# Split-heads rotary embedding: the cos table loaded from SyncE's queue, and TensorE's wait for sin moved behind the spreading of cos

## The chip, the cores and the metric

The kernel runs on one core of a Trainium2 chip. The metric is the device time of one execution in microseconds (us). The engines are TensorE (PE), VectorE (DVE), ScalarE (ACT), GpSimd (POOL) and SyncE (SP); ScalarE and SyncE each have a DMA queue here, which the profile calls q10 and q1, and both are served by the same 16 DMA engines.

## What is computed

```python
def reference(x, cos, sin, num_heads):          # x: 16 x 512 x 1024, cos and sin: 512 x 32, 16 heads
    x = x.reshape(batch, seq, num_heads, head_dim)             # head_dim 64
    x1, x2 = x[..., :half_dim], x[..., half_dim:]              # half_dim 32
    cos, sin = cos[None, :, None, :], sin[None, :, None, :]
    return np.concatenate([x1 * cos - x2 * sin, x1 * sin + x2 * cos], axis=-1)
```

All is float32. 33.55 MB of x are read and as much is written; each of the two tables has 64 KB.

## The kernel before

The 8192 rows of x (batch times sequence) are cut into eight tiles of 1024 rows. A tile has 128 partitions with eight consecutive rows each, 4 MB in all. A step u of the kernel treats one row of each partition, 128 x 1024 numbers, so there are 64 steps. The tiles live in a ring of 40 such rows in SBUF (x_sb, 160 KB of a partition); tiles 5 to 7 reuse the places of tiles 0 to 2, and the results overwrite x in place before they are stored.

For a step, VectorE multiplies x by cos into PSUM (t1_ps, line 347). GpSimd, for most steps, multiplies x with its halves swapped by the sines, the first half with its sign changed, into SBUF (t2_sb, lines 303 and 305); for some steps VectorE does this too (line 340). The sum of the two is made in one of two ways, set by the list PE2: VectorE adds them (line 356), or TensorE adds t2 to t1 in PSUM by a matmul with the identity (line 265) and ScalarE copies the result back (line 227).

Each engine has its own program, and semaphores join them. **ScalarE** (lines 205 to 232) issues the DMA of the first half tile of x (2 MB), then those of cos and sin, then five more x loads: the second half of tile 0 and tiles 1 to 4. It then forms the selection matrix (line 215) from an identity that GpSimd makes, and later the sine tables (lines 222, 223). The loads of tiles 5 to 7 (`late`) are issued by ScalarE behind fixed steps (BEHIND) and wait until the stores of the rows that they overwrite have landed. **SyncE** (lines 195 to 203) issues nothing but the ten stores: each waits for the sums of its rows. **TensorE** (lines 234 to 273) first writes zeros to its banks, then waits for the selection, for cos and for sin, and spreads the two tables with the selection, so that each of the 128 partitions has the table rows of its eight rows: the cos group goes to tab_ps, the sin group to a bank of t1_ps (line 248). One increment of sem_t follows both groups. VectorE's first product, ScalarE's sine copies and through them GpSimd's first product wait for it. There is one tile size, so SIZES has a single entry.

The spreading loop, which fixes the order of the two groups:

```python
for n in SIZES:
    for c, to in enumerate((c_ps[n], raw_sin[n])):
        for k in range(n // R1):
            ins = pe.matmul(...)
    ins.then_inc(sem_t, 1)
```

Of the kernel before, what the change touches and what calls it, by code (L numbers as in the profile page):

```python
# [6 lines left out]
def bass_split_heads_rope_kernel(  # L7
# [14 lines left out]
    R1 = seq // P  # L22
# [27 lines left out]
    SIZES = sorted({t[0] for t in TILES})  # L50
# [40 lines left out]
    with ExitStack() as stack:  # L91
        x_sb = stack.enter_context(nc.sbuf_tensor([P, RING, H, 2, HALF], fp32))
        t2_sb = stack.enter_context(nc.sbuf_tensor([P, NT2, H, 2, HALF], fp32))
        stage = stack.enter_context(nc.sbuf_tensor([P, 2, R1 * HALF], fp32))
# [13 lines left out]
        sem_cos = stack.enter_context(nc.semaphore("cos"))  # L108
        sem_sin = stack.enter_context(nc.semaphore("sin"))
# [37 lines left out]
        def in_dram(flat, t, o, m):  # L147
            n = TILES[t][0]
            run = flat[first_row[t] * P:(first_row[t] + n) * P, :].rearrange("(p r) d -> p (r d)", r=n)
            return run[:, o * dim:(o + m) * dim]  # L150

        def place_of(u):
            t, r = rows[u]
            return TILES[t][1] + r

        def in_sbuf(t, o, m):
            k = TILES[t][1] + o
            return x_sb[:, k:k + m].rearrange("p n h t d -> p (n h t d)")
# [14 lines left out]
        def wait_added(eng, u):  # L173
            if n_pe[u]:
                eng.wait_ge(sem_a, n_pe[u])
            if n_comb[u]:
                eng.wait_ge(sem_v, n_comb[u])  # L177
# [9 lines left out]
        def load(eng, i):  # L187
            t, o, m = loads[i]
            eng.dma_start(in_sbuf(t, o, m), in_dram(xf, t, o, m)).then_inc(sem_in[i], 16)  # L189

        def wait_landed(eng, t, r):
            if (t, r) in load_at:
                eng.wait_ge(sem_in[load_at[t, r]], 16)

        def on_sync(sp):
            for u in range(NU):
                if u not in store_after:
                    continue
                k = store_after[u]
                t, o, m = stores[k]  # L200
                wait_added(sp, u)
                sp.dma_start(in_dram(of, t, o, m), in_sbuf(t, o, m)).then_inc(sem_out.get(k, sem_rest), 16)
            sp.wait_ge(sem_rest, 16 * (len(stores) - len(awaited)))

        def on_scalar(ae):
            early = [i for i in range(len(loads)) if i not in late]
            for i in early:
                load(ae, i)
                if i == 0:
                    for c, (table, sem) in enumerate(((cos, sem_cos), (sin, sem_sin))):  # L210
                        ae.dma_start(stage[:, c, :], table.rearrange("(s r) d -> s (r d)", r=R1)).then_inc(sem, 16)  # L211
            ae.wait_ge(sem_i, 2)
            for n in SIZES:
                m = n // R1
                ae.activation(  # L215
                    pick[n][:],
                    ident[:].rearrange("q (s k) -> q k s", k=m)[:, :, None, :].broadcast_to([P, m, m, P // m]),
                    COPY,
                ).then_inc(sem_g, 1)
            for i, n in enumerate(SIZES):  # L220
                ae.wait_ge(sem_t, i + 1)
                ae.activation(s_sb[n][:, :, 0, :], raw_sin[n], COPY, scale=-1.0)  # L222
                ae.activation(s_sb[n][:, :, 1, :], raw_sin[n], COPY).then_inc(sem_s, 1)  # L223
            for u in range(NU):
                if PE2[u]:
                    ae.wait_ge(sem_e, n_pe[u])
                    ae.activation(xs[:, place_of(u), :], t1_ps[:, u % NT1, :], COPY).then_inc(sem_a, 1)  # L227
                for i in late:
                    if BEHIND[i] == u:
                        for j in TILES[loads[i][0]][4]:  # L230
                            ae.wait_ge(sem_out[j], 16)
                        load(ae, i)

        def on_tensor(pe):
            pe.wait_ge(sem_z, 1)
            for k in range(NT1):
                for b in range(EH):
                    pe.matmul(  # L238
                        t1_ps[:, k, b * BANK:(b + 1) * BANK], zero[:, 0:P], zero[:], start=True, stop=True
                    ).then_inc(sem_w, 1)  # L240
            pe.wait_ge(sem_g, len(SIZES))
            pe.wait_ge(sem_cos, 16)
            pe.wait_ge(sem_sin, 16)
            pe.wait_ge(sem_w, NT1 * EH)
            for n in SIZES:
                for c, to in enumerate((c_ps[n], raw_sin[n])):
                    for k in range(n // R1):
                        ins = pe.matmul(  # L248
                            to[:, k * R1:(k + 1) * R1, :].rearrange("p r d -> p (r d)"),
                            pick[n][:, k].rearrange("q b s -> q (b s)"),  # L250
                            stage[:, c, :],
                            start=c == 0,
                            stop=True,
                            skip_group_check=c == 1,
                        )
                ins.then_inc(sem_t, 1)
            for u in range(NU):
                if not PE2[u]:
                    continue
                if TWO[u - 1]:  # L260
                    pe.wait_ge(sem_q[(u - 1) % NT2], made[u - 1])
                pe.wait_ge(sem_q[u % NT2], made[u])
                t2 = t2_sb[:, u % NT2, :, :, :].rearrange("p h t d -> p (h t d)")
                for b in range(EH):
                    ins = pe.matmul(  # L265
                        t1_ps[:, u % NT1, b * BANK:(b + 1) * BANK],
                        ident[:],
                        t2[:, b * BANK:(b + 1) * BANK],
                        start=False,
                        stop=True,  # L270
                        skip_group_check=True,
                    )
                ins.then_inc(sem_e, 1)
# [40 lines left out]
        def on_vector(ve):  # L314
# [48 lines left out]
            for u in range(NU + LEAD):  # L363
# [6 lines left out]
                if u >= LEAD and not ahead and not PE2[u - LEAD]:  # L370
                    comb(u - LEAD)

        on_sync(nc.sync)
        on_scalar(nc.scalar)
        on_gpsimd(nc.gpsimd)
        on_tensor(nc.tensor)
        on_vector(nc.vector)

# [32 lines left out]
```

## Time and profile before

| what | value |
|---|---|
| time, median of 3 runs | 160.91 us (160.89 to 161.15) |
| the profiled execution: time | 161.04 us |
| its span, first to last instruction | 159.8 us |
| DVE busy | 134.1 us (84%) |
| POOL busy | 126.5 us (79%) |
| PE busy | 56.3 us (35%) |
| ACT busy | 21.8 us (14%) |
| moved by DMA | 67.25 MB, mean 421 GB/s |

A profile comes from one execution, so its durations belong to 161.04 us. Busy time counts instructions of an engine; issuing a DMA and waiting for a semaphore are not counted. The row of 40 digits for an engine shows the busy tenths of 40 equal slices of the span, some 4 us each; the DMA row shows the mean of the 16 DMA engines in the same way. In lines of the timeline the columns are start, duration, engine, line, operation, output and inputs, number of instructions, and in brackets the idle time of the engine before them with what ended it. An "ACTq" or "SPq" line is the issue of a DMA on that engine's queue, not the transfer. The time from issue to landing holds the wait behind other transfers. The trace also records each DMA packet with its start and duration, and when each transfer's semaphore was raised.

### The profile page before, as it was taken

How to read it: one execution, taken by the hardware profiler on the slowest of the kernel's cores; microseconds unless marked ns; L12 is line 12 of the kernel's file. 1: busy time of each engine (PE TensorE's matmuls, PEld its weight loads, DVE VectorE, ACT ScalarE, POOL GpSimd, SP SyncE). 2: the span in 40 equal slices, each digit the busy share in tenths (PEclk: the TensorE clock that was granted, in tenths of full speed). 3: DMA queues.
4: the chain of work that ended last, by engine and by line, in shares of the span. 5: the costliest groups of instructions: out<-in, count | busy, mean ns of one | idle time of the engine just before them, and what ended most of it. 6: DMA issues, size and time to landing. Idle time of an engine off the chain costs nothing.

```text
span 159.8 us, 449 instructions
## 1 busy us (share of the span) xinstructions
PE 56.3 (35%) x90; PEld 19.6 (12%) x90; DVE 134.1 (84%) x121; ACT 21.8 (14%) x23; POOL 126.5 (79%) x40
## 2 busy tenths in 40 slices
PE   6050007744407740788066407740575000000000
PEld 1040002111102110222021102110220000000000
DVE  0028997999999999998999999999799987999500
ACT  0410000331300330022203300330022000000000
POOL 1009999999999999999999999956999289990000
PEclk9999999999985899557659985899557655555555
DMA  5999998999999999999999999999999999999996
GB/s 172 418 426 459 435 476 336 422 414 418 500 406 455 435 427 394 420 492 402 394 500 410 402 484 427 402 427 484 402 394 509 402 402 476 435 402 443 406 439 287
DMA packets 3025, 67.25 MB, mean 421 GB/s; under 512 B 336, under 2 KB 592, under 8 KB 592
## 3 DMA queue, kind: packets, MB, share of 16 engines
q10 hardware_dynamic: 1584, 33.69, 49.8%
q1 hardware_dynamic: 1440, 33.56, 48.8%
q14 instruction: 1, 0.01, 0.0%
HBM read 33.69 MB, written 33.55 MB: 421 GB/s over the span
## 4 chain that ended last, share of the span: by engine, by line
DMA 45%; DVE 34%; POOL 11%; PE 1%; issue 1%; ACTq 1%; ACT 0%; SPq 0%; POOLq 0%
DMA x_sb<-in_x_dram 21%; DMA out_dram<-x_sb 20%; DVE t_ps L347 18%; DVE x_sb L356 14%; POOL t_sb L305 6%; POOL t_sb L166 5%; DMA stage<-in_sin_dram 4%; DVE t_sb L166 3%; PE tab_ps L248 1%; PE t_ps L248 1%; ACTq L211 0%; ACT sine L222 0%; ACTq L189 0%; ACT sine L223 0%; SPq L177 0%
## 5 line engine op out<-in xcount | busy, mean ns | idle before, releaser
L305 POOL TENSOR_TENSOR t_sb<-x_sb,sine 128x2048 f32<-128x2048 f32 x22 | 99.0, 4524 | 6.6 <-DMA x_sb<-in_x_dram 6.6
L347 DVE TENSOR_TENSOR t_ps<-x_sb,tab_ps 128x1024 f32<-128x1024 f32 x64 | 76.8, 1221 | 11.3 <-PE t_ps L248 9.9
L265 PE MATMUL t_ps<-t_sb,ident 128*128 128x512 f32 x76 | 51.5, 818 | 59.4 <-DVE t_ps L347 38.6
L356 DVE TENSOR_TENSOR x_sb<-t_ps,t_sb 128x1024 f32<-128x1024 f32 x45 | 54.7, 1219 | 3.7 <-POOL t_sb L305 3.0
L166 POOL TENSOR_TENSOR t_sb<-x_sb,sine 128x1024 f32<-128x1024 f32 (+1 forms) x12 | 27.6, 2307 | 10.4 <-ACT sine L223 10.4
L227 ACT ACTIVATE x_sb<-t_ps 128x1024 f32<-128x1024 f32 x19 | 19.4, 1023 | 91.9 <-PE t_ps L265 89.9
L265 PEld LDWEIGHTS t_ps<-t_sb,ident 128*128 128x128 f32 x76 | 17.1, 250 | 92.7 <-issue 53.6
L166 DVE TENSOR_TENSOR t_sb<-x_sb,tab_ps 128x1024 f32<-128x1024 f32 (+1 forms) x9 | 10.1, 1124 | 0.0
L238 PE MATMUL t_ps<-zero 128*128 128x512 bf16 x6 | 2.7, 630 | 1.3 <-DVE zero L315 1.3
L248 PE MATMUL tab_ps<-stage,chosen 128*128 128x128 f32 x4 | 1.2, 454 | 4.9 <-DMA stage<-in_sin_dram 4.9
L215 ACT ACT_TABLE_LOAD x1 | 1.3, 1283 | 4.8 <-issue 4.8
L248 PEld LDWEIGHTS tab_ps<-stage,chosen 128*128 128x128 f32 x4 | 0.9, 322 | 5.8 <-issue 5.8
L248 PE MATMUL t_ps<-stage,chosen 128*128 128x128 f32 x4 | 1.1, 421 | 0.0
L315 DVE MEMSET zero<- 128x256 uint32 x1 | 0.3, 272 | 0.9 <-PEq L393 0.9
L238 PEld LDWEIGHTS t_ps<-zero 128*128 128x128 bf16 x6 | 0.7, 137 | 2.4 <-DVE zero L315 1.2
L222 ACT ACTIVATE sine<-t_ps 128x256 f32<-128x256 f32 x1 | 0.4, 383 | 4.4 <-PE t_ps L248 4.4
L248 PEld LDWEIGHTS t_ps<-stage,chosen 128*128 128x128 f32 x4 | 1.0, 333 | 0.0
L276 POOL MEMSET ident<- 128x128 f32 x1 | 0.2, 204 | 0.3 <-POOLq L393 0.3
L215 ACT ACTIVATE chosen<-ident 128x256 f32<-128x256 f32 x1 | 0.4, 429 | 0.0
L223 ACT ACTIVATE sine<-t_ps 128x256 f32<-128x256 f32 x1 | 0.4, 378 | 0.0
L278 POOL TENSOR_SCALAR_AFFINE_SELECT ident<-ident 128x128 f32<-128x128 f32 x1 | 0.3, 292 | 0.1
L393 POOL MEMSET const-float32-0.0<- 128x1 f32 x1 | 0.1, 98 | 0.3 <-issue 0.3
(5 smaller groups left out, 0.7 us busy)
## 6 DMA issues: line engine op xcount, KB each, us to landing
x_sb<-in_x_dram ACTq DMA_DIRECT2D x7, 4096.0 KB, 33.2
out_dram<-x_sb SPq DMA_DIRECT2D x6, 4096.0 KB, 30.2
out_dram<-x_sb SPq DMA_DIRECT2D x4, 2048.0 KB, 16.4
x_sb<-in_x_dram ACTq DMA_DIRECT2D x2, 2048.0 KB, 9.4
stage<-in_cos_dram ACTq DMA_DIRECT2D x1, 64.0 KB, 7.2
stage<-in_sin_dram ACTq DMA_DIRECT2D x1, 64.0 KB, 7.0
```

Source lines behind the costliest of these rows:

```text
L166: return eng.tensor_tensor(t2_sb[:, u % NT2, a:b, :, :], swapped(place_of(u))[:, a:b], table[:, None, :, :].broadcast_to([P, b - a, 2, HALF]),
L215: ae.activation(pick[n][:], ident[:].rearrange("q (s k) -> q k s", k=m)[:, :, None, :].broadcast_to([P, m, m, P // m]), COPY,).then_inc(se ...
L222: ae.activation(s_sb[n][:, :, 0, :], raw_sin[n], COPY, scale=-1.0)
L223: ae.activation(s_sb[n][:, :, 1, :], raw_sin[n], COPY).then_inc(sem_s, 1)
L227: ae.activation(xs[:, place_of(u), :], t1_ps[:, u % NT1, :], COPY).then_inc(sem_a, 1)
L238: pe.matmul(t1_ps[:, k, b * BANK:(b + 1) * BANK], zero[:, 0:P], zero[:], start=True, stop=True).then_inc(sem_w, 1)
L248: ins = pe.matmul(to[:, k * R1:(k + 1) * R1, :].rearrange("p r d -> p (r d)"), pick[n][:, k].rearrange("q b s -> q (b s)"), stage[:, c, :] ...
L265: ins = pe.matmul(t1_ps[:, u % NT1, b * BANK:(b + 1) * BANK], ident[:], t2[:, b * BANK:(b + 1) * BANK], start=False, stop=True, skip_group ...
L278: pl.affine_select(out=ident[:], in_=ident[:], compare_op=mybir.AluOpType.is_equal, fill=0.0, base=0, pattern=[[-1, P]], channel_multiplier=1,
L305: pl.tensor_tensor(t2_sb[:, u % NT2:u % NT2 + 2].rearrange("p n h t d -> p (n h) t d"), x_sb[:, k:k + 2, :, ::-1, :].rearrange("p n h t d ...
L347: ve.tensor_tensor(t1_ps[:, u % NT1, :].rearrange("p (h d) -> p h d", d=HALF), x_sb[:, k, :, :, :].rearrange("p h t d -> p (h t) d"), c_ps ...
L356: ve.tensor_tensor(xs[:, place_of(u), :], t1_ps[:, u % NT1, :], t2_sb[:, u % NT2, :, :, :].rearrange("p h t d -> p (h t d)"), add,).then_i ...
```

## The change

The helper load_table issues the DMA of one table. SyncE calls it for cos before its loop of stores. ScalarE issues only sin behind the first half tile of x. TensorE still waits for the selection, for cos and for its zeros before the first group, but for sin only ahead of the second group. Semaphores, sizes, the order of x loads and of stores, and all arithmetic stay.

```diff
+        def load_table(eng, c):
+            table, sem = ((cos, sem_cos), (sin, sem_sin))[c]
+            eng.dma_start(stage[:, c, :], table.rearrange("(s r) d -> s (r d)", r=R1)).then_inc(sem, 16)
+
         def on_sync(sp):
+            load_table(sp, 0)
             for u in range(NU):
                 if u not in store_after:
                     continue
@@ on_scalar
             for i in early:
                 load(ae, i)
                 if i == 0:
-                    for c, (table, sem) in enumerate(((cos, sem_cos), (sin, sem_sin))):
-                        ae.dma_start(stage[:, c, :], table.rearrange("(s r) d -> s (r d)", r=R1)).then_inc(sem, 16)
+                    load_table(ae, 1)
@@ on_tensor
             pe.wait_ge(sem_g, len(SIZES))
             pe.wait_ge(sem_cos, 16)
-            pe.wait_ge(sem_sin, 16)
             pe.wait_ge(sem_w, NT1 * EH)
             for n in SIZES:
                 for c, to in enumerate((c_ps[n], raw_sin[n])):
+                    if c == 1 and n == SIZES[0]:
+                        pe.wait_ge(sem_sin, 16)
                     for k in range(n // R1):
```

## Prediction

> **What bounds the kernel now.** I read the page's slices and queue table first, then busy time in short windows, then the timeline of the first 12 us, then the waits for x late in the run. The page says that the DMA engines are full nearly from end to end.
>
> ```profile
> span 159.8 us, 449 instructions
> ...
> DVE  0028997999999999998999999999799987999500
> ACT  0410000331300330022203300330022000000000
> POOL 1009999999999999999999999956999289990000
> ...
> DMA  5999998999999999999999999999999999999996
> ...
> q10 hardware_dynamic: 1584, 33.69, 49.8%
> q1 hardware_dynamic: 1440, 33.56, 48.8%
> ```
>
> Queue q10 is ScalarE's (loads), q1 SyncE's (stores). Together they fill 98.6% of 159.8 us on 16 engines: 157.6 us, so an engine is idle for 2.2 us on the mean. VectorE, busy 134.1 us, does nothing in the last 9. Where the 2.2 us lie is shown by the windows (columns: stretch, its length, busy of PE, PEld, DVE, ACT, POOL, granted clock, DMA share, GB/s).
>
> ```profile
> 0.00:2.00 2.00, 0.75 (x2) 0.28 (x3) 0.27 (x1) 0.00 (x0) 0.70 (x6) 1.00 0.45 90
> 2.00:4.00 2.00, 1.99 (x5) 0.45 (x3) 0.00 (x0) 0.00 (x0) 0.00 (x0) 1.00 0.68 254
> 4.00:6.00 2.00, 0.00 (x0) 0.00 (x0) 0.00 (x0) 1.18 (x1) 0.00 (x0) 1.00 1.04 442
> ...
> 150.00:154.00 4.00, 0.00 (x0) 0.00 (x0) 0.02 (x1) 0.00 (x0) 0.00 (x0) 0.50 1.02 438
> 154.00:158.00 4.00, 0.00 (x0) 0.00 (x0) 0.00 (x0) 0.00 (x0) 0.00 (x0) 0.50 0.97 414
> 158.00:160.00 2.00, 0.00 (x0) 0.00 (x0) 0.00 (x0) 0.00 (x0) 0.00 (x0) 0.50 0.33 139
> ```
>
> Nothing moves before 1.82 us, when the first packet of the first x load starts (packet records of the trace); by 4 us the engines run at 430 GB/s, and they do so until 158. After the last arithmetic at 150.0 us DMA is still full: the last store, issued at 150.10, stands behind the one before, which lands at 154.93, and itself lands at 159.76, a time of 4.83 us for 2 MB. So the end is set by when the DMA engines start, by 67.25 MB, and by what they lose on the way. The page's chain of waits runs through VectorE for a third of the span, but it names what came last, and the windows show that an earlier store would find the engines occupied.
>
> **The change, part by part.** Durations are of the profiled execution: span 159.8, time 161.04, so 1.25 us lie outside the span. Its time is 0.13 above the median 160.91.
>
> The start today, from the timeline:
>
> ```profile
> 0.80 0.38 ACTq L189 DMA_DIRECT2D x_sb<-in_x_dram  x1
> 1.21 0.46 ACTq L211 DMA_DIRECT2D stage<-in_cos_dram  x1
> 1.69 0.45 ACTq L211 DMA_DIRECT2D stage<-in_sin_dram  x1
> 2.17 2.62 ACTq L189 DMA_DIRECT2D x_sb<-in_x_dram  x5
> 4.82 1.28 ACT L215 ACT_TABLE_LOAD   x1 [4.82 <-issue]
> 6.12 0.43 ACT L215 ACTIVATE chosen<-ident 128x256 f32<-128x256 f32 x1
> 8.90 1.19 PE L248 MATMUL tab_ps<-stage,chosen 128*128 128x128 f32 x4 [4.91 <-DMA stage<-in_sin_dram]
> 9.89 1.06 PE L248 MATMUL t_ps<-stage,chosen 128*128 128x128 f32 x4
> 10.98 0.38 ACT L222 ACTIVATE sine<-t_ps 128x256 f32<-128x256 f32 x1 [4.44 <-PE t_ps L248]
> 11.79 8.72 POOL L166 TENSOR_TENSOR t_sb<-x_sb,sine 128x1024 f32<-128x1024 f32 x4 [10.43 <-ACT sine L223]
> ```
>
> (a) **ScalarE issues one DMA less**: 0.48 us (1.21 to 1.69). Sin, five x loads, the table load and the spread of the selection move up by it: the selection is ready at 6.55 - 0.48 = 6.07. The x loads behind the first only queue earlier behind full engines: 0.
>
> (b) **SyncE issues cos first.** SyncE is released with the others (0.72 us) and has nothing to do until its first store at 21.81, so its 0.46 us cost no work. The first x packet started 1.02 us after its issue began; cos, issued at 0.80, should start at 1.82 to 1.90, beside x. Its cost to DMA: the 256 packets of 512 B of both tables took 27 ns each, so cos takes 128 x 27 / 16 = 0.22 us of each engine, wherever it stands. Taken before or between x packets instead of behind them: 0.
>
> What the trace of before does not show is two queues that open at the same moment. Best case: cos fills time that the engines lose at the start anyway. The 16 first packets start between 1.82 and 2.87 (mean 2.05) and the packets before 4 us take 0.65 us per engine above the steady 0.611 us for 16 KB; all of this saved would be -0.65. Worst case: the first x load waits for the whole cos issue, +0.46. A second row bounds a queue that opens: around the first store, in 24 to 26 us, load packets took 0.31 us per engine longer than the steady 1.213 us; the two together would be +0.77. I take 0, because the nearest row, the tables' own 0.22 us, only changes place, and the costs of opening exist once already.
>
> (c) **TensorE's wait for sin moves behind the cos matmuls.** The cos group (1.19 us) can run from 6.1, or from when cos lands, at latest some 7 us (eight packets on each engine, alternating with x packets of 0.61 us, from 1.9), and ends by 8.2. Sin still stands behind 2 MB of x in q10, so it lands at 8.65, as today, or up to 0.22 earlier. Behind the new wait are queued the four sin matmuls and then all adds of TensorE; VectorE's first product waits for them too. From 8.65: 0.25 to the matmul, 1.06 for the group, 0.02, two copies to 0.66 later, 0.14 to GpSimd: its first product starts at 10.8, not 11.79. VectorE moves from 11.09 to 10.1. **The front of the arithmetic gains 1.0 us**, the cos group that no longer stands behind sin; the first store is issued at 20.8, not 21.81.
>
> (d) **Where that 1.0 us goes.** Loads and stores share full engines, so a store that starts earlier takes time from the loads. Stores in q1 wait for one another: the store issued at 63.65 lands at 95.19, behind the one that lands at 75.76, so issuing it 1.0 earlier moves little. Its landing releases the last x load (issued 95.21, landed 128.35). GpSimd already waits for late loads:
>
> ```profile
> 109.07 4.51 POOL L305 TENSOR_TENSOR t_sb<-x_sb,sine 128x2048 f32<-128x2048 f32 x1 [3.01 <-DMA x_sb<-in_x_dram]
> ...
> 128.42 4.51 POOL L305 TENSOR_TENSOR t_sb<-x_sb,sine 128x2048 f32<-128x2048 f32 x1 [3.56 <-DMA x_sb<-in_x_dram]
> ```
>
> The gain becomes a longer wait there, and what got past it would meet the backlog of stores. At the end: 0. If that cover were gone, -1.0. The order of the mid-run packets can shift the other losses of the trace (0.31 at 24 to 26, 0.25 at 34 to 36): 0, plus or minus 0.3.
>
> Sum: 161.04 + 0 (a) + 0 (b) + 0 (c, d) = 161.04; on the median, which is 0.13 lower, **160.9**.
>
> A rule weighed against this, in sentences that the sum does not use: the Trainium skill, DMA: Bandwidth & Descriptors, section Bandwidth, gives a 64 KB transfer 0.95 us, as dominated by its descriptors. If cos cost that between x loads today, taking it out of the way would save up to 0.95 and give about 160.0. The trace disagrees: 27 ns per packet, 0.22 us in all.
>
> **The rivals.** Two tenths of a per cent, 0.32 us, is about what a measurement of this kernel can tell from no change.
>
> *The head shortens.* Cos draws the first slow accesses and fills the uneven start. For: 0.65 us is lost there. Against: both queues are released together, so x pays its own first access. Price -0.22 (cos hidden) to -0.65, middle -0.4: **160.5**. Chance 0.15.
>
> *The arithmetic is the bound after all*: -1.0 reaches the end, **159.9**. For: the chain gives VectorE 34%. Against: DMA share 1.02 and 0.97 after the arithmetic has ended, and the waits above. Chance 0.04.
>
> *Slower: the descriptors of cos go out ahead of those of x.* The place is the first x load; the price is the 0.46 us of the cos issue, as every later packet stands behind: **161.4**. It decides the case when the mean first x packet moves from 2.05 to beyond 2.37. For: SyncE and ScalarE are released 5 ns apart and each issue took 0.33 to 0.56 us. Against: cos would move in part of that time. Chance 0.15. The Trainium skill, DMA: Bandwidth & Descriptors, section Queues, rings and completion order, supports it: SP and ACT each own a ring on the same engines but no descriptor generator of their own. No run yet shows two issues at once.
>
> *It doesn't do what it says*: cos queues so long behind x packets that it lands with sin, as the first store's first packet came 4.4 us after its issue. Then the 1.0 us at the front shrinks, and the end stays at **160.9**. Chance 0.08.
>
> *Some other order of late loads opens a gap in DMA*: 161.3 or more, chance 0.04.
>
> **How the numbers follow.** The forecast has 0.54. Same within 0.2%: 0.54 + 0.08 = 0.62. Faster: 0.15 + 0.04 = 0.19. Slower: 0.15 + 0.04 = 0.19. The range runs from 160.5 (head shortened by its middle price) to 161.4 (cos issue charged whole); outside lie the compute case, the remainder of the last one, and the far parts of the head's bounds, together under 0.2.
>
> **What the profile after should show.** First x packet at 1.8 to 1.9 and about 172 GB/s in the first slice. Cos on SPq, issued near 0.8. TensorE's cos group from 6.1 to 7, its sin group at 8.5 to 8.9, VectorE's first product at 10.1, GpSimd's at 10.8, the first store near 20.8. Then the proof of (d): the last two x loads still land within 0.3 us of 109.0 and 128.35, GpSimd's waits there grow towards 4.0 and 4.6, DMA stays at 9 in every slice between the first and the last, and the last store lands at 159.8 within 0.3. The prediction is wrong if the first x packets move by over 0.3 us, if DMA shows a gap, or if the last landing follows the arithmetic by its 1.0 us.

## The result and the profile after

The changed kernel takes **162.62 us** (median of 4 runs, 162.56 to 162.82), the kernel before on the same chip 160.95. The ratio is 1.0101, 95% interval 1.0089 to 1.0113: **1% slower**. The forecast was 160.9, no change, with a range up to 161.4. The profiled execution took 162.82 us with a span of 161.6, so the span grew by 1.76 us.

The page of the kernel after, its span, its DMA slices and its queues:

```profile
span 161.6 us, 448 instructions
...
DMA  5999999999999999999999999999999999999995
...
q10 hardware_dynamic: 1440, 33.62, 49.6%
q1 hardware_dynamic: 1584, 33.62, 48.4%
```

The engines are as full as before. There is no gap, and the time is longer all the same: the bytes are unchanged, so the engines moved them more slowly (mean 416 GB/s, before 421). The start of the kernel after, from its timeline:

```profile
0.80 0.39 ACTq L189 DMA_DIRECT2D x_sb<-in_x_dram  x1
0.80 0.38 SPq L197 DMA_DIRECT2D stage<-in_cos_dram  x1
...
1.22 0.46 ACTq L197 DMA_DIRECT2D stage<-in_sin_dram  x1
...
6.52 1.19 PE L253 MATMUL tab_ps<-stage,chosen 128*128 128x128 f32 x4 [2.52 <-DMA stage<-in_cos_dram]
...
8.57 1.22 PE L253 MATMUL t_ps<-stage,chosen 128*128 128x128 f32 x4 [0.86 <-DMA stage<-in_sin_dram]
...
9.93 2.36 DVE L352 TENSOR_TENSOR t_ps<-x_sb,tab_ps 128x1024 f32<-128x1024 f32 x2 [8.74 <-PE t_ps L253]
...
10.64 4.65 POOL L166 TENSOR_TENSOR t_sb<-x_sb,sine 128x1024 f32<-128x1024 f32 x2 [9.27 <-ACT sine L227]
```

All of this went as the change means it to: cos spread at 6.5, sin at 8.6, VectorE 1.16 us earlier than before (11.09), GpSimd 1.15 us earlier (11.79). The first store is issued at 20.65 instead of 21.81. Up to here nothing is slower: the second half tile of x lands at 13.38 (before 13.49), tile 1 at 23.09 (23.20). Tile 2 is the first that lands later (37.51 against 37.02); by then the stores run beside the loads, and the first store lands earlier (40.74 against 41.86). The last two x loads in GpSimd's timeline of the kernel after:

```profile
111.36 4.50 POOL L310 TENSOR_TENSOR t_sb<-x_sb,sine 128x2048 f32<-128x2048 f32 x1 [4.11 <-DMA x_sb<-in_x_dram]
...
131.29 4.51 POOL L310 TENSOR_TENSOR t_sb<-x_sb,sine 128x2048 f32<-128x2048 f32 x1 [4.13 <-DMA x_sb<-in_x_dram]
```

GpSimd waits for data that come 2.3 us (111.36 against 109.07) and 2.9 us (131.29 against 128.42) later than before. That is more than the whole run lost: loads share the engines with stores that now start earlier, and tile 2 was late by 0.5 us before any of the new losses below. One stretch of the run, busy time and DMA by windows (last columns: granted clock, DMA share, GB/s), first the kernel before, then the kernel after:

```profile
66.00:126.00 60.00, 31.05 (x44) 10.05 (x42) 58.43 (x52) 11.26 (x11) 55.85 (x14) 0.73 0.99 429
```

```profile
66.00:126.00 60.00, 29.96 (x42) 9.59 (x40) 55.54 (x49) 11.26 (x11) 53.58 (x14) 0.76 1.00 424
```

A share of 1.00 with 424 GB/s instead of 429: packets take longer. A busy row of DMA can't show this; the packet records can. In steady state a packet of 32 KB takes 1.213 us, one of 16 KB 0.611, so each microsecond above that is a loss that can be placed. Summed and divided by 16 engines:

| above the steady packet, us per engine | before | after |
|---|---|---|
| 0 to 4 us (start; with 0.09 after for cos's packets, above 27 ns) | 0.65 | 0.41 |
| 20 to 40 us (stores begin) | 0.65 | 0.56 |
| after 66 us | 0.02 | 1.26 |
| mean end of the 16 engines | 158.87 | 159.96 |
| end of the last engine | 159.41 | 161.18 |

The mean end moved by 1.09 us, and the last engine falls behind that mean by 1.22 us instead of 0.54. Together, 1.77, this is the 1.76 us of the span. The new loss lies almost wholly (1.23 of the 1.26 us) in load packets, at three places: 72.9 to 76.9, 92.5 to 96.8 and 112.3 to 116.6 us. Those are the moments at which the stores of tiles 1, 2 and 3 end (72.8 to 75.1, 92.3 to 94.8, 112.0 to 114.7).

The records don't name the engine of a packet. But in steady state each packet starts within 4 ns of the end of another, and an engine takes eight packets of each x load and of each store, so the packets can be strung into 16 chains, one for each engine. A typical chain from 63 us on, with L a load packet, S a store packet, `|l` and `|s` the end of an x load and of a store, and +n the ns above the steady duration:

```
before   S L S L S |l S L S L |s L S L S L S L S L S
after    L S L S L S |l S L |s L S L+511 S L S L S L
```

Before, the store ends two load packets after the load. After, it ends one load packet after, and one or two of the load packets behind it are slow. That order goes back to the start of the stores: on 14 of 16 engines three load packets of tile 2 ran before the first store packet (four on the others), and after the change two on 13 engines and three on the rest. From there on the two queues alternate, and the distance stays.

The chains also limit this reading. In the changed kernel the three engines with three packets ahead lost no less than the thirteen with two: 1.73 us after 66 us on their mean, against 1.15. And at 53 to 55 us, where the last store of tile 0 ends (in packets of 16 KB), the thirteen engines already have the distance of one load packet, and no load packet behind it is slow. So the distance alone, on one engine, does not make the cost.

### The profile page after: what moved, and what is told of

The parts are those of the page before. It is cut to its first block, busy times and chain, and to the rows that moved or that the text cites. A ratio compares the mean times of both kernels' runs of the same rounds, so it can differ in the third digit from the quotient of the medians.

```text
span 161.6 us, 448 instructions
## 1 busy us (share of the span) xinstructions
PE 57.6 (36%) x90; PEld 20.1 (12%) x90; DVE 134.3 (83%) x121; ACT 21.8 (14%) x23; POOL 126.6 (78%) x40
## 4 chain that ended last, share of the span: by engine, by line
DMA 47%; DVE 33%; POOL 11%; issue 1%; PE 1%; ACT 0%; ACTq 0%; SPq 0%; POOLq 0%
DMA x_sb<-in_x_dram 23%; DMA out_dram<-x_sb 20%; DVE t_ps L352 18%; DVE x_sb L361 13%; POOL t_sb L310 6%; POOL t_sb L166 5%; DMA stage<-in_sin_dram 5%; DVE t_sb L166 3%; PE t_ps L253 1%; ACTq L189 0%; ACT sine L226 0%; ACT sine L227 0%; SPq L177 0%; POOLq L301 0%
## 5 line engine op out<-in xcount | busy, mean ns | idle before, releaser
L270 PE MATMUL t_ps<-t_sb,ident 128*128 128x512 f32 x76 | 52.5, 833 | 60.3 <-DVE t_ps L352 37.3
L166 DVE TENSOR_TENSOR t_sb<-x_sb,tab_ps 128x1024 f32<-128x1024 f32 (+1 forms) x9 | 10.1, 1124 | 0.0
```

Of the source, the lines that this page charges most:

```text
L166: return eng.tensor_tensor(t2_sb[:, u % NT2, a:b, :, :], swapped(place_of(u))[:, a:b], table[:, None, :, :].broadcast_to([P, b - a, 2, HALF]),
L270: ins = pe.matmul(t1_ps[:, u % NT1, b * BANK:(b + 1) * BANK], ident[:], t2[:, b * BANK:(b + 1) * BANK], start=False, stop=True, skip_group ...
```

## The experiments

**Theory A**: the 1.1 us that the arithmetic gains makes the stores begin earlier in the stream of loads, so that later the ends of loads and stores fall one load packet apart, and there load packets are slow. **Theory B**: cos in SyncE's queue is itself what costs. Theory C: the head of the x loads.

The results in one table. Every kernel was timed beside the kernel before on its own chip. "Ahead" is the number of tile 2's load packets ahead of the first store packet (engines in brackets); the loss is that after 66 us. Issue, order and loss come from one profiled execution each, the times from all runs; the profiled executions of e2 and e10 took 161.65 and 161.47 us, more than their medians.

| kernel | first store issued | ahead | loss per engine | us, median | ratio to before, 95% |
|---|---|---|---|---|---|
| before | 21.8 | 3 (14), 4 (2) | 0.02 | 160.95 | |
| after | 20.65 | 2 (13), 3 (3) | 1.26 | 162.62 | 1.0101 (1.0089 to 1.0113) |
| e1, both waits first | 21.8 | 3 (14), 4 (2) | 0.03 | 161.16 | 1.0013 (1.0003 to 1.0023) |
| e2, store 0 held 1.1 | 21.75 | 3 (15), 2 (1) | 0.08 | 161.23 | 1.0020 (1.0007 to 1.0034) |
| e3, cos first on ScalarE | 21.1 | 2 (14), 3 (2) | 1.15 | 163.18 | 1.0144 (1.0124 to 1.0164) |
| e4, before, store 0 held | 22.8 | 4 (14), 3 (2) | 0.05 | 161.04 | 1.0003 (0.9994 to 1.0012) |
| e5, store 0 held 0.6 | 21.3 | 3 (10), 2 (6) | 0.49 | 161.81 | 1.0044 (1.0031 to 1.0056) |
| e6, store 0 held 2.2 | 22.8 | 4 (15), 3 (1) | 0.03 | 161.02 | 0.9999 (0.9990 to 1.0009) |
| e7, store of tile 1 held | 20.8 | 2 (11), 3 (5) | 0.04 | 161.06 | 1.0008 (0.9996 to 1.0021) |
| e8, other rows in HBM | 20.6 | 2 (16) | 0.74 | 162.84 | 1.0101 (1.0075 to 1.0127) |
| e9, split wait alone | 21.45 | 3 (12), 2 (4) | 0.22 | 161.93 | 1.0057 (1.0040 to 1.0075) |
| e10, both tables on SyncE | 23.7 | 4 (8), 5 (8) | 0.15 | 160.96 | 0.9997 (0.9988 to 1.0007) |
| e11, store 0 held 3.8 | 24.4 | 5 (14), 6 (2) | 0.03 | 161.03 | 1.0003 (0.9994 to 1.0012) |

**e1**, the change with the wait put back ahead of both groups:

```diff
             pe.wait_ge(sem_cos, 16)
+            pe.wait_ge(sem_sin, 16)
...
-                    if c == 1 and n == SIZES[0]:
-                        pe.wait_ge(sem_sin, 16)
```

> The changed kernel with part (c) undone: cos still loaded by SyncE, but TensorE waits for cos and sin ahead of both groups. The first store should be issued near 21.7 us, as in the kernel before (21.81), not at 20.65. Theory A (the arithmetic's lead of 1.1 us moves the stream of stores against the stream of loads, and the DMA engines lose time where the two meet): about 160.9, and no slow load packets near 74, 94 and 114 us. Theory B (having cos in SyncE's queue is itself what costs, at the head or by the place of later packets in the queues): stays at 162.6. Theory C (the head of the x loads): stays at 162.6 too, but the first x load landed 0.1 us later only, and sin and all loads up to 23 us earlier than before, so C is unlikely.

161.16, and hardly a slow packet after 66 us. Cos on SyncE's queue is in this kernel too, with the uneven start, so theories B and C fall as causes of the 1.67 us; some 0.2 us (interval 1.0003 to 1.0023) stay unexplained. The start even loses less (0.34 us per engine above the steady packet, before 0.65).

**e2**, the whole change, only its first store held (e5, e6 and e11 with 1, 4 and 8 copies instead of 2; e4 the same on the kernel before):

```diff
                 wait_added(sp, u)
+                if k == 0:
+                    sp.wait_ge(sem_d, 2)
@@ on_scalar, ahead of its loop of steps
+            wait_added(ae, 3)
+            for i in range(2):
+                if i:
+                    ae.wait_ge(sem_d, i)
+                ae.activation(pick[8][:], ...same input as at the first use..., COPY).then_inc(sem_d, 1)
```

> The changed kernel, whole, with only its first store held back by about 1.05 us (two small extra copies on the idle ScalarE, then SyncE may issue), to 21.7 us. The arithmetic keeps its lead. Theory A, with the first store as the lever: 160.9 to 161.2. If the lead of the arithmetic itself or that of the later stores matters, or theory B: 162.6.

Holding one store by 1.1 us takes back 1.4 of the 1.67 us, with the arithmetic's lead untouched. The single chain that still had two load packets ahead lost 0.85 us after 66 us and ended last, at 160.04, where 14 of the others ended by 158.91: the profiled span of 160.4 is that one engine's. Here the cost fell on the engine that kept the order of the change.

**e3**, cos as ScalarE's first DMA, ahead of x, with the split wait:

```diff
         def on_sync(sp):
-            load_table(sp, 0)
@@ on_scalar
+            load_table(ae, 0)
             for i in early:
```

> Cos is issued by ScalarE as its first DMA, ahead of x; SyncE issues stores only; TensorE's wait for sin stays split. x starts about 0.46 us later, so sin should land near 8.9 to 9.1 and the lead of the arithmetic should be 0.6 to 0.8 us, with the first store near 21.0. Theory A: slower than before, 161.5 to 163 (0.2 to 0.5 for the late head, the rest from the meeting of the streams). Theory B: at most 161.4, the late head alone.

163.18, above the range that theory A named (to 163). SyncE issues no table here, and the slow packets are there: B is out from this side too. Some 0.3 us are the late head: the second half tile, with both tables and the first half ahead of it as before, lands at 13.82 (before 13.49). The rest is the loss after 66 us and the last engine, which ends 1.4 us behind the mean. As in the change, the few engines with three packets ahead are not spared: the two lost some 1.9 us each, the fourteen 1.0 on the mean.

**e4**, the kernel before with its first store held to 22.8:

> The kernel before with only its first store held back by about 1.05 us, to 22.9 us. Theory A says that the time depends on when the stores begin: it should move by some tenths at least, in either direction (160.3 to 162.6), and the slow packets should differ in place from those of before. Theory B: 160.9 within 0.2.

Theory A's expectation failed: I had expected some tenths either way, and nothing moved. Four packets ahead are as good as three: from an issue at 21.8 us on, the time no longer follows the store's start.

**e5**, half of the way:

> The changed kernel with its first store held by about 0.5 us, to 21.2 us: half of the way back. Theory A in its sharper form (what counts is how many load packets of 32 KB each DMA engine takes from tile 2 before its first store packet: three or more in the kernel before and where the store was held, two in the changed kernel): some engines have two and some three, so 161.2 to 162.6, with a wide scatter of runs and of the engines' ends. A theory in which the cost grows smoothly with the lead gives 161.9.

161.81 with a mixed order: ten engines with three packets, six with two. In this kernel both groups lost after 66 us: the six some 0.8 us each, the ten some 0.3. So the loss falls on the engines with two packets above all, and reaches the others too when enough have two. A half-way time would have come out of a smooth theory as well; e4 and e6 exclude one in which the time goes on falling past 21.8 us, and e7 any that rests on the first store alone.

**e6**, held by about 2 us:

> The changed kernel with its first store held by about 2.0 us, to 22.7 us. Sharper theory A: all engines have three or four load packets of tile 2 ahead, no slow load packets after 60 us, the engines end within 0.8 us of each other, 160.5 to 161.0, at least as fast as the kernel before. Smooth theory: 160 or less. If an early arithmetic has a cost of its own: over 161.2.

161.02, level with the kernel before. The arithmetic still leads by 0.9 us (GpSimd starts at 10.87), and the lead is worth nothing at the end: DMA sets it.

**e7**, the store of tile 1 held instead, the first two as early as in the changed kernel:

```diff
                 wait_added(sp, u)
+                if k == 2:
+                    sp.wait_ge(sem_v, n_comb[u] + 2)
```

> The changed kernel with its first two stores as early as there (20.65 and 31.6 us) and only the third store (tile 1) held from 46.65 to about 53.4 us, so that SyncE's queue runs dry for two or three packets and the later ends of stores fall further behind the ends of loads. If the meeting of load and store ends late in the run costs (theory A in its place): no slow load packets after 66 us and 160.9 to 161.4, though the first store is early. If the early first store costs by its own start: 162.6.

This separates the early start from the later distance. The first store is early (20.8) and its start loses as much as ever (0.67 us at 20 to 40). SyncE's queue then runs dry for two to four load packets, and the stores end three or four load packets behind the loads:

```
e7, a chain from 52 us      L |s L L L L S L S L S L S |l S L S L S L S L |s L S L S
```

The slow packets are all but gone (0.04 us per engine) and the time is 161.06. The windows of this kernel show the rate of the kernel before:

```profile
66.00:126.00 60.00, 30.58 (x42) 9.64 (x41) 56.49 (x50) 11.26 (x11) 55.02 (x14) 0.73 1.00 431
```

431 GB/s, where the change had 424. So the cost lies where the ends of loads and stores meet late in the run, not in the early store as such.

**e8**, other addresses for the stores of tiles 1 to 6:

```diff
+        spare = nc.dram_tensor("spare", [batch * seq + 64, dim], fp32, kind="Internal").ap()[24:24 + batch * seq, :]
...
-                sp.dma_start(in_dram(of, t, o, m), ...)
+                sp.dma_start(in_dram(spare if 0 < t < 7 else of, t, o, m), ...)
```

> The changed kernel, but the stores of tiles 1 to 6 go to a spare tensor in HBM, 24 rows (96 KB) from its start, and not to the output; these rows of the output are left unwritten. Sizes, order, issue times as in the changed kernel. If the slow load packets come from reads and writes that meet in HBM at the same offsets of a tile: they vanish or change, 161.0 to 161.5. If they come from the order of packets on the engines alone: 162.6 and slow packets at the same places, near 74, 94 and 114 us.

162.84, the ratio of the change, though this kernel leaves the rows of tiles 1 to 6 in the output unwritten. So the cost doesn't need the stores to go to the same offsets as the loads. One other place was tried, and it changed the form: the loss after 66 us is 0.74 us per engine instead of 1.26, but the last engine ends at 161.37, 2.1 us behind the mean (159.23). The rows in SBUF stayed the same.

**e9**, part (c) alone, both tables on ScalarE's queue:

```diff
             pe.wait_ge(sem_cos, 16)
-            pe.wait_ge(sem_sin, 16)
...
+                    if c == 1 and n == SIZES[0]:
+                        pe.wait_ge(sem_sin, 16)
```

> Part (c) alone on the kernel before: both tables still behind the first half tile of x in ScalarE's queue, TensorE's wait for sin moved behind the cos group. Cos lands only 0.22 us ahead of sin, so the lead of the arithmetic is 0.1 to 0.2 us and the first store is issued near 21.6 to 21.7. Theory A: three load packets of tile 2 ahead of the first store packet on nearly every engine, 160.9 to 161.3. If the moved wait by itself costs: 162 and more.

161.93, not 160.9 to 161.3: cos landed 0.21 us ahead of sin as expected, but the first store came 0.36 us earlier (21.45), and four engines slipped to two packets. Those four lost 0.86 us on the mean after 66 us (0.44 to 1.29), the other twelve 0.00; two of the four ended at 160.06 and 160.08, all others by 159.31. The kernel before stands near the edge of the costly order: a third of a microsecond is enough for a quarter of the engines.

**e10**, sin on SyncE's queue too:

```diff
             load_table(sp, 0)
+            load_table(sp, 1)
@@ on_scalar
-                if i == 0:
-                    load_table(ae, 1)
```

> The changed kernel with sin, too, loaded by SyncE, right behind cos. Both tables should land by 7, the first products then wait for x (8.3 to 8.5), and the first store should be issued near 19 to 19.5, over 2 us earlier than before. Theory A: one load packet or less of tile 2 ahead of the first store packet. If nearness of the two ends is what costs, whichever comes first: 162 to 163.5. If only the order 'load ends, then store, one packet later' costs: back to 161. No gain from the earlier arithmetic in either case: not below 160.5.

My expectation of when sin lands was wrong. It came at 11.55 us, not by 7, as TensorE's wait in this kernel's timeline shows:

```profile
11.59 1.23 PE L252 MATMUL t_ps<-stage,chosen 128*128 128x128 f32 x4 [3.87 <-DMA stage<-in_sin_dram]
```

Each engine's eight small packets alternate with x packets of 0.611 us: cos landed at 6.44, and sin needed some 5.1 us more (eight turns of 0.64). So the arithmetic was late by 1.9 us instead of early, the first store came at 23.7 and the time is 160.96. The question that the run was meant for, whether one packet or none ahead also costs, was not answered.

**e11**, the first store held by about 4 us:

> The changed kernel with its first store held by about 4 us, to 24.7 us: five or six load packets of tile 2 ahead of the first store packet. Theory A: no slow load packets after 60 us, 160.7 to 161.1, as with 2 us. If stores that begin late cost in the end (the last tiles then wait for their places): over 161.3.

161.03. From three packets on, more distance brings nothing, and a first store issued as late as 24.4 us doesn't cost. None of the twelve versions beats the kernel before by more than the intervals allow.

## Why the prediction was wrong

It was right in (a), (b) and (c) up to the first store. VectorE began at 9.93 (predicted 10.1), GpSimd at 10.64 (10.8), the cos group at 6.52 (6.1 to 7), the sin group at 8.57 (8.5 to 8.9), the first store was issued at 20.65 (20.8). The bounds on two queues that open together were not needed: x's first packets did begin 0.37 us later on the mean (2.42 against 2.05), which was the sign named for the slower rival, and yet the second half tile landed 0.11 us earlier, since the start lost less on the packets themselves. So the first half of that rival occurred, and its price did not: no late head reached the loads behind. That the 161.4 of this rival was the nearest to the result is chance. The rule of the Trainium skill named beside it (DMA: Bandwidth & Descriptors, section Queues, rings and completion order: no descriptor generator for each issuing engine) would fit the later first packet, but it cost nothing here. The prediction also named a move of the first x packets by over 0.3 us as a sign of being wrong; the sign came, but not for the cause that it stood for.

It was right in (d) that full engines leave nothing of the arithmetic's gain at the end: e6 has the lead and the time of before. That GpSimd's waits came out near the forecast (4.0 and 4.6, measured 4.11 and 4.13) is luck: they were to grow while the last two x loads still landed within 0.3 us of 109.0 and 128.35, and these landed at 111.29 and 131.22.

**The step that failed is the last one of (d)**: "The order of the mid-run packets can shift the other losses of the trace (0.31 at 24 to 26, 0.25 at 34 to 36): 0, plus or minus 0.3." The term was mis-sized. It measured 1.24 us per engine after 66 us (less 0.33 gained in the first 40, plus 0.18 that is left, about what the engines start later), and 0.68 us more because the engines came apart and the last one sets the end. Two conditions were taken for granted there. The first was that engines that are full all the time move bytes at one rate: the rate fell from 429 to 424 GB/s with the share at 1.00. The second was that the packet order of the kernel before was indifferent, when it was one packet from a bad one. Its trace had the means to ask: load packets took up to 0.5 us longer at the two places where the stores began to mix in, 24 to 26 and 34 to 36 us, and hardly any after 40, which says that the mixing can cost. The rival "some other order of late loads" looked for a gap in DMA, with a chance of 0.04 and 161.3 us or more; what came was no gap but slow packets.

**What stays open** is why load packets are slow when a store ends one load packet after a load. The runs show that the cost all but goes when no engine, or only one, has this distance late in the run (e2, e6, e7, e11), that cos's queue is not needed (e3, e9), and that another place in HBM for the stores doesn't remove it (e8). Where few engines have the distance, they bear the loss (e2, e9); where most have it, the others lose as much (the change, e3). It is not enough by itself, as the end of tile 0's stores shows. Whether the descriptors, the two memories or the engine's own turn between its queues make it was not settled: no run moved the rows in SBUF that are read and written side by side, none tried a distance of no load packet, and none a store that ends ahead of the load.

## What to carry to other kernels

In this kernel, whose DMA engines are full from end to end, an earlier first result bought nothing and cost 1%: it moved the stores against the loads, and the order that the engines then took was a worse one. The same can be asked of any kernel whose DMA share stays at 1.00. Look at packet durations and at the ends of single engines, not only at the DMA share, before calling such a shift neutral; the last of 16 engines set the end here. If a change makes the arithmetic earlier in such a kernel, hold the first store where it was and see whether the time comes back: one added wait is the whole test.

## What the runs showed of the hardware

- Packets of an x load took 1.213 us in steady state on every engine, and up to 0.6 us longer in the changed kernel (56 of them by over 0.1 us) at three moments when on most engines a store ended one load packet after a load; this cost 1.24 us per engine. In the seven kernels in which no engine had that distance then, the loss after 66 us was 0.02 to 0.15 us per engine.
- The engines came apart with it: they ended within 0.74 us of each other before, within 2.25 us after.
- From the issue of the first store to its first packet passed 4.4 us before (21.81 to 26.22) and 4.1 us after (20.65 to 24.72), with nothing ahead of it in its own queue. At the start 1.0 us passed from an issue to the first packet; the other 3.1 to 3.4 us are, by estimate, some three load packets of 1.213 us that the full engines had still to finish.
- A 64 KB table on a queue of its own landed 5.6 us after its issue beside a bulk load, and a second one behind it at 11.55 us, which fits small packets that each wait their turn behind a packet of 0.611 us (eight turns of 0.64 are 5.1 us). Behind 2 MB in the bulk queue, sin landed at 8.65: for the second table the crowded queue was the faster one.
